# Where experts without tokens among the first 256 stand in the order of a streamed mixture of experts

## The chip, the cores and the metric

One NeuronCore of a Trainium2 chip runs the whole program. The metric is device microseconds of one execution. Beside the plain runs there is one profiled execution, whose trace gives the start and end of every instruction, what each waited for, and every DMA packet.

## The reference

One residual block over 512 tokens of width 1024, in float32. After a token mixer and a LayerNorm a hierarchical mixture of experts follows: a router picks one of 4 groups, then 2 of that group's 8 experts, so 1024 assignments fall on 32 experts.

```python
pg = softmax(xt @ w_rg + b_rg);  grp = argmax(pg)
le = (xt @ w_re + b_re).reshape(n_tok, 4, 8)[grp]
top_v, top_i = lax.top_k(le, 2)
gate = p_grp * softmax(top_v)
eid = grp * 8 + top_i
...
hb = silu(xb @ w1[e]) * (xb @ w3[e])      # w1, w3: 1024 x 512
y  = (hb @ w2[e]) * gate                  # w2: 512 x 1024, added to the token's row
out = LN2(alpha * h + sum of the two y)
```

The setup scales the router's biases up (`b_rg` by 185, `b_re` by 61), so the load is uneven. Evaluating the reference's router on its own inputs gives these tokens per expert (rows are groups, columns experts 0 to 7 of a group):

```
all 512 tokens                    first 256 tokens
 1   0   2   2   1   2   1   1     0   0   1   2   1   1   1   0
57  55  40  18  94  83  37 130    29  30  16  11  40  36  16  62
34  22  82 104  15  18 126  19    18  12  43  54   5  12  65   5
 0  11   8   5  26  15  13   2     0   7   5   4  17   8  11   0
```

Experts 1 and 24 get no token at all. Experts 0, 7 and 31 get none among the first 256, but one, one and two later.

## The kernel before, in words

Up to about 690 us the token mixer, the residual, the first LayerNorm and the router run. From there to the end the 32 experts are taken one after the other, each as one "block" b = 0 to 31; the position in the order is the block's number.

**Weights.** A block needs six chunks of 1 MB (128 partitions x 8 KB): chunks 0 to 3 hold w1 and w3, chunks 4 and 5 hold w2. `load_big` (L402) issues each chunk as one DMA from SP's queue into a ring of 17 buffers (12 named `raw`, then `rawl`, `raw`, `rawl`, `rawh`, `rawh`; in the trace a run of twelve `raw` loads is followed by these five). The queue's sequence is (b; 0 to 3), (b-1; 4, 5), (b+1; 0 to 3), (b; 4, 5) and so on. From block 3 on a load carries a condition: if the expert's final count is zero, the instruction is issued, but moves nothing.

**Lanes.** Each DMA from SP or ACT is given one of eight semaphores, in turn, by the framework (`DMAHW0` to `DMAHW7` below; I call them lanes). A DMA waits until the one before it on its lane has landed, whichever queue that one was issued from. A skipped load takes its lane and gives it back at once.

**A block.** `run` (L1393) does, in step b: `up` (L1539, h = x w1 and x w3), `gate` (L1546 on ACT, L1547 on DVE), `turn_x` of block b+1 (L1514), `down` of block b-1 (L1567), `turn` of block b (L1553 to L1557), `store_y` of block b-1 (copies L1594 and L1599, scatters L1574 on POOL). `up` and `down` are in branches on the token count: a 32-row part runs if a remainder is left (`xs`), and one or two 64-row parts (`x`) if the count is above 32 or 96. A block without tokens still goes through its transposes, gate, copies and scatters.

**The tail.** From position 25 (`RT`) on, four of the 17 buffers are taken out of the ring and used for the last LayerNorm. In step 25, behind the copies of `turn`, ACT issues four 4 KB loads of LayerNorm rows (L1622) on lanes 5, 6, 0 and 1. In step 29 ACT issues the first of four 1 MB loads of finished rows (L1689) behind all scatters so far; these take lanes 4, 6, 3 and 5.

**The order.** It is made on the chip, from the counts of the first 256 tokens (`order`, L1118), before the second half of the router has run. Every expert gets a key; its position is the number of smaller keys. The keys' parts are `seq` (group + 4 x index in the group, times 8 + 1/64, which takes the groups in turn), minus the count, and three bands: experts 0, 8 and 16 first, whatever their counts; those with tokens next; those without tokens; and last the four held for the end (`lt`, of each group the one with the fewest tokens among those that have any), whose rows go straight into the last LayerNorm.

Of the kernel before, what the change touches and what calls it, by code (L numbers as in the profile page):

```python
# [22 lines left out]
OP = mybir.AluOpType  # L23
# [5 lines left out]
T, D, NT, KD, H = 512, 1024, 4, 8, 8  # L29
E, FE = 32, 512  # L30
# [24 lines left out]
def bc(ap, n, at):  # L55

    dims = [list(d) for d in ap.ap]
    dims.insert(at, [0, n])
    return bass.AP(tensor=ap.tensor, offset=ap.offset, ap=dims)
# [201 lines left out]
class K:  # L261
# [4 lines left out]
    def consts(self, S, M, W):  # L266


        nc, a, c = self.nc, self.a, {}
        self.c = c  # L270
        v, g = nc.vector, nc.gpsimd
# [6 lines left out]
        def iota(pool, name, shape, pat, base, cm):  # L278
            t = pool.tile(shape, F32, name=name)
            g.iota(t, pattern=pat, base=base, channel_multiplier=cm, allow_small_or_imprecise_dtypes=True)  # L280
            return t
# [64 lines left out]
        q = c["seq"].rearrange("p (g j) -> p g j", g=4)  # L346
        v.tensor_scalar(c["seq"], c["seq"], 8.0 + 1.0 / 64, None, op0=OP.mult)
        v.tensor_scalar(q[:, 0:NPRE, 0:1], q[:, 0:NPRE, 0:1], -1e4, 1e3, op0=OP.add, op1=OP.mult)
        iota("jx", [128, E], [[0, 4], [1, 8]], 0, 0)
        c["onesx"] = c["ones"][:, 0:NX * E]  # L350
        c["ones_bf"] = S.tile([128, 128], BF, name="ones_bf")
        v.memset(c["ones_bf"], 1.0)
# [722 lines left out]
class Router:  # L1075
# [42 lines left out]
    def order(self):  # L1118


        nc, W, cst, v, g = self.nc, self.W, self.cst, self.nc.vector, self.nc.gpsimd
        for t in range(2):
            q = W.tile([128, 2, E], BF, name="oq")
            v.tensor_tensor(out=q, in0=bc(cst["iota"][:, 0:E], 2, 1), in1=bc(self.ek[:, :, t], E, 2), op=OP.is_equal)
            for k in range(2):
                nc.tensor.matmul(self.cps[:, NT], cst["ones_bf"], q[:, k], start=t + k == 0, stop=t + k == 2)
        gj = lambda x: x.rearrange("p (g j) -> p g j", g=4)
        f = W.tile([128, E], F32, name="of_")
        v.tensor_scalar(f, self.cps[:, NT], 0.0, None, op0=OP.is_gt)
        v.memset(gj(f)[:, 0:NPRE, 0:1], 1.0)  # L1130
        sc = W.tile([128, E], F32, name="os_")
        v.scalar_tensor_tensor(out=sc, in0=self.cps[:, NT], scalar=32.0, in1=cst["jx"], op0=OP.mult, op1=OP.add)
        ne = W.tile([128, E], F32, name="on_")
        v.tensor_scalar(ne, f, -1e6, 1e6, op0=OP.mult, op1=OP.add)
        v.tensor_tensor(out=sc, in0=sc, in1=ne, op=OP.add)
        v.memset(gj(sc)[:, 0:NPRE, 0:1], 2e6)
        mn = W.tile([128, 4], F32, name="om_")
        v.tensor_reduce(out=mn, in_=gj(sc), axis=AX.X, op=OP.min)
        lt = W.tile([128, E], F32, name="ol_")
        v.tensor_tensor(out=gj(lt), in0=gj(sc), in1=bc(mn, 8, 2), op=OP.is_equal)  # L1140
        v.scalar_tensor_tensor(out=lt, in0=sc, scalar=1e6, in1=lt, op0=OP.is_lt, op1=OP.mult)
        v.scalar_tensor_tensor(out=f, in0=f, scalar=-1024.0, in1=cst["seq"], op0=OP.mult, op1=OP.add)
        v.tensor_tensor(out=f, in0=f, in1=self.cps[:, NT], op=OP.subtract)
        v.scalar_tensor_tensor(out=f, in0=lt, scalar=4096.0, in1=f, op0=OP.mult, op1=OP.add)
        eq = W.tile([128, E, E], BF, name="oeq")
        v.tensor_tensor(out=eq, in0=bc(f, E, 1), in1=bc(f, E, 2), op=OP.is_lt)
        pos = W.tile([128, E], F32, name="op_")
        v.tensor_reduce(out=pos, in_=eq, axis=AX.X, op=OP.add)
        v.tensor_tensor(out=eq, in0=bc(pos, E, 1), in1=bc(cst["iota"][:, 0:E], E, 2), op=OP.is_equal)
        g.tensor_tensor(out=eq, in0=eq, in1=bc(cst["iota"][:, 0:E], E, 1), op=OP.mult)  # L1150
        v.tensor_reduce(out=self.ord, in_=eq, axis=AX.X, op=OP.add)
        v.tensor_copy(out=self.ordi, in_=self.ord)
# [833 lines left out]
```

## Time and profile before

| | |
|---|---|
| median of 3 runs | 1206.45 us (1206.35 to 1207.39) |
| profiled execution | 1204.72 us, of which the span from first to last instruction is 1202.9 us |
| instructions | 18,914 |
| granted TensorE clock, mean of the span | 0.938 |
| PE, DVE, ACT, POOL busy | 87%, 55%, 33%, 19% of the span |
| weight loads of the experts issued by L402 | 192 (of which 12 are skipped) |
| matmul records of `up`, 32-row parts | 1120 + 192 + 160 = 1472, that is 64 each for 23 blocks |
| matmul records of `up`, 64-row parts | 352 + 64 + 32 = 448, that is 32 each for 14 parts |

The counts of records agree with the table of tokens above: 23 experts have a remainder for the 32-row part, 8 have one 64-row part and 3 have two. Busy shares are means over stages with different limits; what the expert stage waits for is read from its own stretch of the trace. "DMA share" there is the mean busy share of the core's 16 DMA engines, and can read slightly above 1.

### The profile page before, as it was taken

The page shows a single profiled execution, that of the slowest core. Times are in us where ns is not written, and L with a number is a line of the kernel's source. Part 1 is how long each engine was busy: PE and PEld are TensorE (multiplying, and loading weights), DVE is VectorE, ACT ScalarE, POOL GpSimd, SP SyncE. Part 2 cuts the span into 40 slices and gives each one's busy share as a digit, 9 for nine tenths or more (in the row PEclk, how much of TensorE's full clock was granted, in tenths as well). Part 3 has the DMA queues.
Part 4 walks back from the last instruction along what each step waited for, and adds up shares of the span by engine and source line. Part 5 has one row for each costly group of instructions (what it writes and reads, how often), then busy time and mean ns, then how long its engine had stood idle before and what let it go on. Part 6 is the DMA issues. An engine that isn't in the chain of part 4 may idle for free. (4 is left out here: it accounts for less than half of the span.)

```text
span 1202.9 us, 18914 instructions
## 1 busy us (share of the span) xinstructions
PE 1045.7 (87%) x6866; PEld 687.0 (57%) x6866; DVE 656.7 (55%) x1392; ACT 401.1 (33%) x849; POOL 230.7 (19%) x296
## 2 busy tenths in 40 slices
PE   3999999999999999999999968888888879767853
PEld 2788688867777777767788633443443334333321
DVE  7566535367586777764485645453333323335584
ACT  6333337335545445444533121121111101122210
POOL 1000100022212322230100123232222212233301
PEclk8999999999999999999999979999989989876767
DMA  4422342621122111111647579999999999987996
GB/s 174 162 70 72 119 144 88 214 84 53 54 70 71 53 53 54 53 54 61 223 159 297 210 287 385 387 401 397 393 399 399 380 408 413 409 328 302 409 407 241
DMA packets 57930, 268.82 MB, mean 223 GB/s; under 512 B 12881, under 2 KB 17265, under 8 KB 33736
## 3 DMA queue, kind: packets, MB, share of 16 engines
q1 hardware_dynamic: 44400, 246.96, 53.8%
q0 software_dynamic: 10224, 10.88, 3.0%
q10 hardware_dynamic: 3176, 9.20, 2.1%
q8 instruction: 87, 1.43, 0.5%
q14 instruction: 43, 0.35, 0.1%
HBM read 274.23 MB, written 27.29 MB: 251 GB/s over the span
## 5 line engine op out<-in xcount | busy, mean ns | idle before, releaser
L215 PE MATMUL psi<-hTh,lo 128*128 128x512 f32 x448 | 183.7, 411 | 1.6 <-DVE lo L215 1.6
L215 PE MATMUL psi<-hTh,hi 128*128 128x512 f32 x448 | 184.2, 414 | 0.9 <-ACT hi L215 0.5
L215 PE MATMUL psi<-hTl,hi 128*128 128x512 f32 x448 | 183.9, 413 | 0.0
L1547 DVE TENSOR_TENSOR h<-h,u 128x640 f32<-128x640 f32 x32 | 26.3, 821 | 245.4 <-ACT h L1546 245.4
L215 DVE TENSOR_TENSOR lo<-raw,hi 128x1024 fp32r<-128x1024 f32 x74 | 92.4, 1249 | 79.8 <-ACT hi L215 79.6
L215 ACT CAST hi<-raw 128x1024 fp32r<-128x1024 f32 x74 | 77.4, 1046 | 108.0 <-PE psi L215 91.1
L1539 PE MATMUL u<-raw,xs 128*32 128x256 f32 x1120 | 79.9, 427 | 30.4 <-DMA raw<-in_w 28.7
L215 PEld LDWEIGHTS psi<-hTh,lo 128*128 128x128 f32 x448 | 84.9, 190 | 21.4 <-issue 3.9
L215 PEld LDWEIGHTS psi<-hTh,hi 128*128 128x128 f32 x448 | 85.1, 190 | 20.2 <-issue 2.6
L215 PEld LDWEIGHTS psi<-hTl,hi 128*128 128x128 f32 x448 | 84.7, 189 | 17.5 <-issue 2.0
L1546 ACT ACTIVATE h<-u 128x640 f32<-128x640 f32 x32 | 22.5, 704 | 200.8 <-PEq L1481 151.9
L1539 PE MATMUL u<-raw,x 128*64 128x512 f32 x352 | 80.8, 608 | 2.5 <-PEq L1479 1.4
L1539 PEld LDWEIGHTS u<-raw,xs 128*32 128x32 f32 x1120 | 37.9, 120 | 65.7 <-DMA raw<-in_w 37.6
L1574 POOL DMA_INDIRECT y_rows<-ysmall,itail x28 | 26.1, 933 | 223.1 <-DVE ysmall L1594 205.9
L1556 ACT COPY hT<-t 128x128 f32<-128x128 f32 x32 | 8.5, 266 | 176.4 <-PE t L1553 176.4
L1574 POOL DMA_INDIRECT y_rows<-ylarge,islot x56 | 57.2, 1022 | 44.4 <-ACT ylarge L1599 31.0
L215 DVE SCALAR_TENSOR_TENSOR acc<-xp,cols,acc 128x512 f32<-128x512 f32 x72 | 54.5, 758 | 5.3 <-ACT acc L215 4.1
L1567 PE MATMUL yz<-raw,hT 128*32 128x256 f32 x560 | 44.7, 459 | 14.3 <-DMA raw<-in_w 5.5
L1539 PEld LDWEIGHTS u<-raw,x 128*64 128x64 f32 x352 | 28.4, 140 | 49.3 <-issue 46.2
L1594 DVE COPY ysmall<-yz 32x256 f32<-32x256 f32 x112 | 46.7, 417 | 6.6 <-PE yz L1567 4.1
L1567 PE MATMUL y<-raw,hT 128*64 128x512 f32 x168 | 39.0, 604 | 7.2 <-PEq L1479 6.9
L1514 PE MATMUL t<-ident,mh 64*128 64x64 f32 x256 | 24.4, 243 | 23.5 <-PEq L1481 19.1
(505 smaller groups left out, 1987.6 us busy)
## 6 DMA issues: line engine op xcount, KB each, us to landing
raw<-in_w SPq DMA_DIRECT2D x144, 1024.0 KB
raw<-in_wt SPq DMA_DIRECT2D x73, 512.0 KB
rawl<-in_w SPq DMA_DIRECT2D x24, 1024.0 KB
rawh<-in_w SPq DMA_DIRECT2D x24, 1024.0 KB
raw<-in_wv SPq DMA_DIRECT2D x8, 512.0 KB
y_rows<-zero SPq DMA_DIRECT2D x8, 512.0 KB
raw<-y_rows ACTq DMA_DIRECT2D x4, 1024.0 KB
rawl<-in_wo SPq DMA_DIRECT2D x3, 1024.0 KB
```

What stands on the lines that cost most here:

```text
L215: op._ins = getattr(getattr(self.nc, op.attr), op.name)(*map(real, op.args), **{k: real(x) for k, x in op.kw.items()})
L1514: nc.tensor.transpose(self.t[0][:, k * NA:k * NA + NA], r[0][:, k * 128:k * 128 + 128], ident[0:NA, 0:NA])
L1539: self.nc.tensor.matmul(self.u[q * r:(q + 1) * r, NP if p is None else p, 0:c], x[:, k, r0:r0 + r], self.raw[b, k // 2][:, o:o + c], start ...
L1546: self.nc.scalar.activation(out=h, in_=u[:, :, 0], func=AF.Silu)
L1547: self.nc.vector.tensor_mul(out=h, in0=h, in1=u[:, :, 1])
L1556: self.nc.scalar.copy(out=x[:, n], in_=self.t[1][:, 0:128])
L1567: self.nc.tensor.matmul(y[q * r:(q + 1) * r, 0:c], t[:, i, j * r:(j + 1) * r], self.raw[b, 4 + k // 2][:, o:o + c], start=k == 0, stop=k == 3)
L1574: x = self.nc.gpsimd.indirect_dma_start(out=out, out_offset=bass.IndirectOffsetOnAxis(ap=idx, axis=0), in_=src, in_offset=None, bounds_che ...
L1594: nc.vector.tensor_copy(out=small[:, q], in_=src)
```

## The change

Experts without tokens among the first 256 lose their band behind the others. They get a key of their own, `apart` = 80.5 + 24.0625 x group + 6 x index, which lies inside the range of the keys of the experts with tokens (`seq` before, 0 to 248.5, less the count). Everything else of the order stays.

```diff
-        iota("jx", [128, E], [[0, 4], [1, 8]], 0, 0)
+        iota("apart", [128, E], [[385, 4], [96, 8]], 1288, 0)
+        v.tensor_scalar(c["apart"], c["apart"], 1.0 / 16, None, op0=OP.mult)
+        v.tensor_tensor(out=c["seq"], in0=c["seq"], in1=c["apart"], op=OP.subtract)
...
-        v.scalar_tensor_tensor(out=sc, in0=self.cps[:, NT], scalar=32.0, in1=cst["jx"], op0=OP.mult, op1=OP.add)
+        v.scalar_tensor_tensor(out=sc, in0=self.cps[:, NT], scalar=64.0, in1=cst["apart"], op0=OP.mult, op1=OP.add)
...
-        v.scalar_tensor_tensor(out=f, in0=f, scalar=-1024.0, in1=cst["seq"], op0=OP.mult, op1=OP.add)
+        v.tensor_tensor(out=f, in0=f, in1=cst["seq"], op=OP.mult)
+        v.tensor_tensor(out=f, in0=f, in1=cst["apart"], op=OP.add)
         v.tensor_tensor(out=f, in0=f, in1=self.cps[:, NT], op=OP.subtract)
```

With the counts above, the order by position is as follows, as expert(tokens of all 512). It was worked out from the formulas of `order`; positions 0 to 9 and 28 to 31 are the same in both.

```
position   before                              now
10 to 13   3(2) 12(94) 4(1) 13(83)             1(0) 3(2) 12(94) 7(1)
14 to 17   28(26) 22(126) 5(2) 21(18)          4(1) 13(83) 28(26) 22(126)
18 to 21   15(130) 29(15) 14(37) 6(1)          24(0) 5(2) 21(18) 15(130)
22 to 25   30(13) 23(19) 24(0) 1(0)            29(15) 14(37) 6(1) 31(2)
26, 27     7(1) 31(2)                          30(13) 23(19)
28 to 31   2(2) 11(18) 27(5) 20(15)            the same
```

On DVE, among the constants at the program's start (`seq` and `apart` are the tables of key parts):

```order
 L215 TENSOR_SCALAR seq<-seq 128x32
 L215 TENSOR_SCALAR seq<-seq 128x3
+L215 TENSOR_SCALAR apart<-apart 128x32
+L215 TENSOR_TENSOR seq<-seq,apart 128x32
 L215 TENSOR_TENSOR ustrict<-uincl,ident 128x128
```

Two instructions came in behind those that make `seq`; those that follow are the same, two places later.

On DVE, in `order`, before (`of_` is the key, `os_` and `om_` the choice of the four held for the end, `cps` the counts; the number behind a name is that of the buffer):

```order
L1129 TENSOR_SCALAR of__5020<-cps_4777 128x32
L1132 SCALAR_TENSOR_TENSOR os__5023<-cps_4777,jx_183 128x32
L1130 MEMSET of__5020 128x3
L1134 TENSOR_SCALAR on__5025<-of__5020 128x32
L1135 TENSOR_TENSOR os__5023<-os__5023,on__5025 128x32
L1142 SCALAR_TENSOR_TENSOR of__5020<-of__5020,seq_182 128x32
L1136 MEMSET os__5023 128x3
L1143 TENSOR_TENSOR of__5020<-of__5020,cps_4777 128x32
L1138 TENSOR_REDUCE om__5029<-os__5023 128x4
```

and now (a line of the changed file is two or three higher):

```order
L1131 TENSOR_SCALAR of__5022<-cps_4779 128x32
L1134 SCALAR_TENSOR_TENSOR os__5025<-cps_4779,apart_183 128x32
L1132 MEMSET of__5022 128x3
L1136 TENSOR_SCALAR on__5027<-of__5022 128x32
L1137 TENSOR_TENSOR os__5025<-os__5025,on__5027 128x32
L1144 TENSOR_TENSOR of__5022<-of__5022,seq_182 128x32
L1138 MEMSET os__5025 128x3
L1145 TENSOR_TENSOR of__5022<-of__5022,apart_183 128x32
L1140 TENSOR_REDUCE om__5031<-os__5025 128x4
L1146 TENSOR_TENSOR of__5022<-of__5022,cps_4779 128x32
```

One instruction more stands in the chain from the counts to the order; the rest keeps its place.

On SP, the weight loads around the four row loads of step 25, before: chunks (26; 1 to 3), (25; 4, 5), (27; 0, 1). What stands in brackets is what the DMA waits for: its lane, and PE, which must have read the buffer's last chunk.

```order
L402 DMA raw_5341<-in_w 128x2048 [waits DMAHW4_49,PE_49]
L402 DMA raw_5342<-in_w 128x2048 [waits DMAHW7_49,PE_49]
L402 DMA raw_5343<-in_w 128x2048 [waits DMAHW2_49,PE_49]
L402 DMA raw_5344<-in_w 128x2048 [waits DMAHW3_49,PE_49]
L402 DMA rawl<-in_w 128x2048 [waits DMAHW4_49,PE_49]
L402 DMA raw_4757<-in_w 128x2048 [waits DMAHW5_49,PE_49]
L402 DMA rawl<-in_w 128x2048 [waits DMAHW6_49,PE_49]
```

and now:

```order
L404 DMA raw_5344<-in_w 128x2048 [waits DMAHW4_49,PE_49]
L404 DMA raw_5345<-in_w 128x2048 [waits DMAHW7_49,PE_49]
L404 DMA raw_5346<-in_w 128x2048 [waits DMAHW2_49,PE_49]
L404 DMA raw_5347<-in_w 128x2048 [waits DMAHW3_49,PE_49]
L404 DMA rawl<-in_w 128x2048 [waits DMAHW4_49,PE_49]
L404 DMA raw_4759<-in_w 128x2048 [waits DMAHW5_49,PE_49]
L404 DMA rawl<-in_w 128x2048 [waits DMAHW6_49,PE_49]
```

Nothing moved here, nor anywhere on PE, ACT, POOL and SP: the program on these engines is the same, and so are its lanes. What moves is the expert that stands at a position, and with it which loads are skipped: chunks of positions 24 and 25 before, of positions 10 and 18 now.

## The prediction

> **What bounds the kernel now.** I read the stretch of the experts first, as a table of windows from 740 us on: busy time of each engine, granted clock, DMA share, GB/s.
>
> ```profile
> core 0: us, PE busy (x) PEld busy (x) DVE busy (x) ACT busy (x) POOL busy (x), PEclk, DMA share, GB/s
> 740.00:1050.00 310.00, 257.72 (x2271) 120.41 (x2271) 107.09 (x218) 50.13 (x99) 83.77 (x86) 0.96 1.02 399
> 1050.00:1055.00 5.00, 2.96 (x34) 1.69 (x35) 2.95 (x6) 0.00 (x0) 0.06 (x1) 0.80 0.97 393
> 1055.00:1060.00 5.00, 4.12 (x53) 1.95 (x51) 1.26 (x3) 1.83 (x4) 2.81 (x3) 0.86 0.85 323
> 1060.00:1065.00 5.00, 2.96 (x36) 1.68 (x40) 1.60 (x4) 0.70 (x1) 1.06 (x2) 0.82 0.94 360
> 1065.00:1070.00 5.00, 3.96 (x29) 1.53 (x21) 2.93 (x6) 0.43 (x2) 0.00 (x0) 0.50 0.56 224
> 1070.00:1075.00 5.00, 1.54 (x16) 1.11 (x20) 1.46 (x4) 2.10 (x4) 3.70 (x4) 0.84 0.84 296
> 1075.00:1080.00 5.00, 3.19 (x33) 1.58 (x25) 3.27 (x7) 0.85 (x2) 0.66 (x2) 0.82 1.01 411
> 1080.00:1085.00 5.00, 1.41 (x9) 1.11 (x9) 1.76 (x4) 1.78 (x3) 3.37 (x4) 0.53 0.46 178
> 1085.00:1090.00 5.00, 4.58 (x37) 2.29 (x40) 3.70 (x7) 1.83 (x4) 1.56 (x2) 0.50 0.09 16
> 1090.00:1140.00 50.00, 40.97 (x350) 18.06 (x343) 25.59 (x37) 12.63 (x24) 18.13 (x17) 0.76 1.01 402
> ...
> 1145.00:1150.00 5.00, 1.88 (x27) 0.84 (x29) 2.38 (x2) 2.11 (x6) 0.00 (x0) 0.85 0.90 339
> 1150.00:1180.00 30.00, 17.85 (x169) 7.36 (x165) 24.10 (x35) 3.72 (x8) 2.74 (x4) 0.61 1.01 421
> ```
>
> The DMA engines are full (1.02 at 399 GB/s) for 310 us, and again from 1090 us on. PE is not: 258 of 310 us. So a weight chunk of 1 MB (1.049 million bytes) takes 1.049/0.399 = 2.63 us, and six of them, 15.8 us, are the price of a block. The one hole of size is 1050 to 1090 us. Next the waits of SP's queue, us in total, times, longest, and its issues of weight loads:
>
> ```profile
> SPq L402 <- DMA raw<-in_w: 194.6, 96, 4.4
> ...
> SPq L402 <- DMA raw<-y_rows: 26.1, 4, 17.5
> SPq L1652 <- DMA raw<-in_w: 19.1, 1, 19.1
> ...
> SPq L402 <- DMA raw<-in_rows: 9.0, 1, 9.0
> ...
> 1015.75 30.09 SPq L402 DMA_DIRECT2D raw<-in_w  x12
> 1048.01 0.09 SPq L402 DMA_DIRECT2D rawl<-in_w  x1
> 1050.48 0.08 SPq L402 DMA_DIRECT2D raw<-in_w  x1
> 1053.56 0.07 SPq L402 DMA_DIRECT2D rawl<-in_w  x1
> 1056.30 2.61 SPq L402 DMA_DIRECT2D rawh<-in_w  x2
> 1061.06 14.09 SPq L402 DMA_DIRECT2D raw<-in_w  x12
> 1078.49 0.08 SPq L402 DMA_DIRECT2D rawl<-in_w  x1
> 1088.62 0.34 SPq L402 DMA_DIRECT2D raw<-in_w  x1
> ...
> 1186.41 2.89 SPq L1652 DMA_DIRECT2D out<-h1s  x4
> ```
>
> SP mostly waits for an earlier weight load to land: its lane. Loads of 0.07 to 0.09 us are skipped ones; 1048.01 is chunk (24, 0). They still wait for their lanes, about 2.6 us each, and put nothing in flight: the reserve of loads under way melts. In the middle of that, SP stands still from 1078.49 to 1088.62, 9.0 us of it for the row loads of step 25, whose lane chunk (27, 0) comes next on. ACT's rows (gates, copies of `turn`, the row load):
>
> ```profile
> 1029.40 0.59 ACT L1557 COPY hT<-t 128x512 f32<-128x512 f32 x1
> ...
> 1056.04 0.59 ACT L1557 COPY hT<-t 128x512 f32<-128x512 f32 x1 [0.53 <-PE t L1555]
> 1062.21 0.70 ACT L1546 ACTIVATE h<-u 128x640 f32<-128x640 f32 x1 [4.62 <-PEq L1481]
> ...
> 1072.86 0.70 ACT L1546 ACTIVATE h<-u 128x640 f32<-128x640 f32 x1 [1.47 <-PEq L1481]
> ...
> 1082.08 0.70 ACT L1546 ACTIVATE h<-u 128x640 f32<-128x640 f32 x1 [0.88 <-PEq L1481]
> ...
> 1086.72 0.59 ACT L1557 COPY hT<-t 128x512 f32<-128x512 f32 x1 [1.21 <-PE t L1555]
> 1086.90 0.49 ACTq L1622 DMA_DIRECT2D raw<-in_rows  x1
> ```
>
> ACT gives out the rows only behind block 25's `turn`. The last weights are seen by SP just before its output store at 1186.41, 16.5 us ahead of the span's end. The load stream sets the end; no load can be saved by an order, but a hole in it can.
>
> **The sum.** It is made against the profiled execution, 1204.72 us (span 1202.9 and 1.8 outside), and carried over to the median of 1206.45, 1.73 above it.
>
> *The hole goes.* Shares missing from 1.02 in the eight windows of 1050 to 1090: 0.05 + 0.17 + 0.08 + 0.46 + 0.18 + 0.01 + 0.56 + 0.93 = 2.44, times 5 us = 12.2 us. (By bytes: 991 GB/s times 5 us missing from 399, over 399: 12.4.) Of these 4.75 lie ahead of 1080, where blocks 24 and 25 are skipped back to back, and 7.45 behind it, where SP stands. Positions 24 and 25 now hold six real loads each, so both parts go: -12.2.
>
> *Two holes come in,* at positions 10 and 18, each alone. Each again lets six lanes go empty, but seven loaded blocks lie between them. No row shows a lone skip. The first skipped block's four chunks alone, 1050 to 1065, cost 0.30 x 5 = 1.5 us; half of the pair's cost is 2.4. I take the middle, 1.9 each: +3.8. The pair's second block ran into a reserve already melted, so 2.4 is more likely too high than too low. A lone skip could cost nothing, if three loads in flight were enough; a gain from it is excluded, since it moves no bytes.
>
> [...]
>
> *The row loads' stop stays, its cover comes back.* Lanes 5, 6, 0 and 1 belong to the rows, so when SP comes to (27, 0) the lanes 2, 3, 4 and 7 carry (26, 2), (26, 3), (25, 4) and (25, 5): four real loads, 4 x 2.63 = 10.5 us of cover. Before, the last two were skipped and DMA ran dry at about 1082 (178/399 x 5 = 2.2 us behind 1080). How long SP will stand is read from blocks before: the six blocks ahead of position 25 are now experts 5, 21, 15, 29, 14 and 6, which stood ahead of position 22 before. Rows issue 0.18 us after the copy's start and SP goes on at 1088.62 - 1086.72 = 1.90 after it. At block 22 that moment is 1056.04 + 1.90 = 1057.94; SP was at (24, 0) at 1048.01, and three loads later, where the lanes would now hold it, at 1055.9: a stop of 2.0 us. At block 20, two behind the expert with 130 tokens, 1031.30 against 1015.75 + 7.9: 7.7 us. Both are under 10.5, so nothing runs dry. Since four loads are under way and not seven, I take 0.5 us (the window at 0.94 lost 0.4). Upper end: 7.7, with 2 us for a `down` of block 24 and 4 us of lateness, and 1 us to start again, less 10.5, is 4.2. Lower end 0.
>
> *The instructions.* Their nearest row is one of the chain itself:
>
> ```profile
> L1142 DVE SCALAR_TENSOR_TENSOR of__5020<-of__5020,seq x1: 183/183/183, 663.8 to 663.8; 128x32 f32<-128x32 f32 x1
> ```
>
> One of about 0.19 us is added in `order`, and two at the start, beside vector work that PE doesn't wait for there; if that cover were gone, 0.4 us. The one in the chain: +0.2, between 0 (the first load by the order issues only some 40 us later) and 0.2.
>
> *PE's work* is the same: an empty block's step costs PE the same at each place. By the gates above the two steps took 10.65 and 9.22 us, against 15.8 us of loads that fall away: after each empty position PE is some 10 us further behind the loads. What takes that up is time in which PE waits for loads, here between 833 and 1050 us:
>
> ```profile
> PE u L1539 <- DMA raw<-in_w: 15.5, 11, 2.3
> ...
> PE yz L1567 <- DMA raw<-in_w: 1.8, 2, 1.4
> PE u L1539 <- DMA rawl<-in_w: 1.7, 1, 1.7
> ```
>
> 19.0 us against 19.9: nearly all is swallowed, and expert 7's small block, now at 13, leaves some 5 us more (15.8 against a step of about 10). So 0, with an upper end in the rivals. The row loads of step 29 held SP for 17.5 us and cost one window at 0.90 (0.6 us); positions 28 to 31 are unchanged, and I leave that.
>
> Sum: -12.2 + 3.8 + 0.5 + 0.2 = -7.7. The profiled execution would be 1197.0, the median **1198.7 us**. Own range: from 1194.2 (all 12.2 gained) to 1206.45 - 12.2 + 4.8 + 4.2 + 0.6 = 1203.9.
>
> **Rivals.**
>
> *The stop isn't covered* (0.13). SP comes to (27, 0) and DMA runs dry for as long as before. For it: four lanes, not eight, feed the engines at that place in any order. Against: the cover of 10.5 us. Then the 7.45 stay, with 3.8 for 4.75 and 0.2: 1205.7, inside 0.2% of before.
>
> *PE comes late, slower than before* (0.07). If none of the two steps' 20 us is taken up, the stop is 2.0 + 20 = 22, and 22 + 1 - 10.5 = 12.5 us run dry where I take 0.5: 1210.7. It gets slower than before once 7.7 + 0.5 us run dry, that is, from a stop of 17.7 us, 16 of the 20 left over. Against it stand the 19.0 us of waits; for it, that many of these lie in the blocks right after the heavy ones, and:
>
> ```profile
> L1539 PE MATMUL u<-raw,xs x1120: 376/379/637, 701.2 to 1174.6; 128*32 128x256 f32 x187
> ...
> 1086.61 5.56 PE L1539 MATMUL u<-raw,xs 128*32 128x256 f32 x64
> ```
>
> Behind the empty steps the granted clock was 0.53 and 0.50, and these 64 matmuls took 5.56 us, which at 376 instead of 637 ns each would be 3.3: up to 2.3 us more per empty position. That is 4.6 us of lateness in all, under the 16 needed. [...]
>
> *The order isn't what I worked out* (0.06). If the counts of the first 256 tokens differ on the chip, the empty positions fall elsewhere; if they stay at the end, nothing is gained: 1206.5. For the counts speak the numbers of matmul records, which come from the same router.
>
> *Lone skips and the stop cost nothing* (0.08): 1194.2 to 1196.
>
> **How the numbers follow.** 0.66 for my forecast, and the rivals as given. About 0.2%, 2.4 us, is what a measurement of this kernel can tell from no change: 1204.0 and 1208.9. My case and the last rival are faster: 0.74. The uncovered stop and the other order are within: 0.19. PE late is slower: 0.07. The range runs from 1194.2 to 1205.7, from the whole hole gained to the uncovered stop.
>
> **What would show it.** In the changed profile SP's loads of under 0.1 us stand near 812 and 934 us and not at 1048 to 1078; the windows there dip for some 15 us by 0.1 to 0.2 and no window after 1050 falls under 0.8 until the last load; the wait for the row loads is still there, up to 8 us, with the share near 1; the output store comes near 1178.7 and the span ends 16.5 us later. I am wrong if SP waits for PE at L402 in 850 to 1050, if a window near 1060 to 1080 falls to 0.5, or if the dips at the two skips cost more than 2.4 us each.

## The result, and the profile after

The changed kernel takes **1197.93 us** (median of 4 runs, 1195.99 to 1199.78) against 1206.4 for the kernel before on the same chip: a ratio of 0.9925, 95% interval 0.9910 to 0.9941. That is 8.5 us less; 7.7 were forecast. The profiled execution took 1195.99 us (span 1194.1, granted clock 0.945). A second chip, on which the kernel before takes 1218.8 us, shows no gain that can be measured; that is the subject of half the experiments.

The windows of the changed kernel in the form of those of before (busy time per engine, granted clock, DMA share, GB/s):

```profile
740.00:1050.00 310.00, 255.57 (x2198) 121.39 (x2195) 111.12 (x226) 51.55 (x101) 86.78 (x89) 0.93 1.02 397
810.00:815.00 5.00, 4.57 (x22) 1.96 (x24) 1.39 (x4) 1.40 (x3) 2.68 (x3) 1.00 1.02 418
...
820.00:825.00 5.00, 5.00 (x30) 2.03 (x26) 0.00 (x0) 0.57 (x1) 0.00 (x0) 1.00 1.02 418
...
1060.00:1065.00 5.00, 4.04 (x25) 1.69 (x25) 3.14 (x7) 0.33 (x2) 0.95 (x2) 1.00 1.01 383
1065.00:1070.00 5.00, 3.49 (x64) 1.82 (x56) 0.00 (x0) 1.64 (x4) 2.79 (x3) 1.00 0.88 318
1070.00:1075.00 5.00, 4.27 (x60) 3.01 (x64) 3.81 (x8) 1.53 (x4) 0.18 (x1) 1.00 1.02 389
1075.00:1080.00 5.00, 3.22 (x54) 1.87 (x46) 1.65 (x3) 1.06 (x2) 3.06 (x4) 1.00 0.77 307
1080.00:1085.00 5.00, 3.69 (x40) 1.67 (x40) 3.00 (x6) 0.70 (x1) 2.86 (x3) 0.78 0.89 331
```

The hole of 12.2 us is gone. What is left of it is 0.14 + 0.25 + 0.13 shares of 5 us, 2.6 us, around the row loads. At and behind the skipped loads the share is 1.02 (first skip); no window of 5 us at the second falls under 0.99.

SP's issues (start, time, engine and line, tensor), from two stretches, and the start of its output store:

```profile
810.18 0.09 SPq L404 DMA_DIRECT2D raw<-in_w  x1
812.66 0.08 SPq L404 DMA_DIRECT2D rawl<-in_w  x1
...
937.59 0.07 SPq L404 DMA_DIRECT2D raw<-in_w  x1
...
1178.78 3.24 SPq L1655 DMA_DIRECT2D out<-h1s  x4
```

The skipped loads (0.07 to 0.09 us) now stand near 812 and 934, and the store at 1178.78, where 1178.7 was forecast. The waits of SP's queue from 740 us on (total, times, longest), and then what PE's own queue waits for between 833 and 1050 us in weight loads, which is all that is left of 19.0 us before:

```profile
SPq L404 <- DMA raw<-in_w: 134.8, 61, 7.8
SPq L404 <- PEq L1484: 53.0, 14, 9.6
...
SPq L404 <- PE y L1570: 15.1, 3, 8.1
...
SPq L404 <- DMA raw<-in_rows: 5.6, 1, 5.6
```

```profile
PE yz L1570 <- DMA raw<-in_w: 0.4, 1, 0.4
```

The same wait of SP for PE's queue before, over the same stretch:

```profile
SPq L402 <- PEq L1481: 18.3, 7, 7.4
```

So PE has changed sides: it no longer waits for weights, and SP now waits for PE to free buffers, 53.0 us at L1484 (18.3 before) and 15.1 at L1570 (0.2 before). The DMA share stays at 0.99 or more up to 1065 us all the same: between 800 and 1050 us a `raw` load took 17.8 us from issue to landing at the median, nearly seven times the 2.64 us that a chunk takes at 397 GB/s, so an estimated six or seven loads were under way.

### The profile page after: what moved, and what is told of

Same layout as the page of the kernel before. It is cut to its first block, busy times and chain, and to the rows that moved or that the text cites. A ratio compares the mean times of both kernels' runs of the same rounds, so it can differ in the third digit from the quotient of the medians.

```text
span 1194.1 us, 18917 instructions
## 1 busy us (share of the span) xinstructions
PE 1043.8 (87%) x6866; PEld 690.0 (58%) x6866; DVE 657.4 (55%) x1395; ACT 401.0 (34%) x849; POOL 230.8 (19%) x296
## 5 line engine op out<-in xcount | busy, mean ns | idle before, releaser
L215 ACT CAST hi<-raw 128x1024 fp32r<-128x1024 f32 x74 | 77.4, 1047 | 108.0 <-PE psi L215 91.3
L1542 PE MATMUL u<-raw,xs 128*32 128x256 f32 x1120 | 78.5, 426 | 16.5 <-DMA raw<-in_w 15.0
L1542 PE MATMUL u<-raw,x 128*64 128x512 f32 x368 | 83.8, 604 | 2.6 <-PEq L1482 1.5
L1549 ACT ACTIVATE h<-u 128x640 f32<-128x640 f32 x32 | 22.6, 705 | 181.4 <-PEq L1484 139.4
L1542 PEld LDWEIGHTS u<-raw,xs 128*32 128x32 f32 x1120 | 41.2, 121 | 47.9 <-DMA raw<-in_w 19.1
L1570 PE MATMUL yz<-raw,hT 128*32 128x256 f32 x560 | 42.2, 439 | 12.9 <-PEq L1522 6.8
L215 POOL TENSOR_TENSOR rk<-ssk,mhalf 128x4 f32<-128x4 f32 x8 | 9.6, 1194 | 183.1 <-DVE ssk L215 168.6
L1570 PE MATMUL y<-raw,hT 128*64 128x512 f32 x152 | 39.7, 666 | 5.8 <-PEq L1482 5.8
```

The costliest lines, as they stand in the source:

```text
L215: op._ins = getattr(getattr(self.nc, op.attr), op.name)(*map(real, op.args), **{k: real(x) for k, x in op.kw.items()})
L1542: self.nc.tensor.matmul(self.u[q * r:(q + 1) * r, NP if p is None else p, 0:c], x[:, k, r0:r0 + r], self.raw[b, k // 2][:, o:o + c], start ...
L1549: self.nc.scalar.activation(out=h, in_=u[:, :, 0], func=AF.Silu)
L1570: self.nc.tensor.matmul(y[q * r:(q + 1) * r, 0:c], t[:, i, j * r:(j + 1) * r], self.raw[b, 4 + k // 2][:, o:o + c], start=k == 0, stop=k == 3)
```

## The experiments

The runs went to chips of two kinds. "The first chip" below stands for those on which the kernel before takes 1206.4 to 1206.7 us, as in the result; on "the second chip" it takes 1218.7 to 1218.8 us. Ratios are always to the kernel before on the same chip.

### The code with the old order; second chip

```diff
-        iota("apart", [128, E], [[385, 4], [96, 8]], 1288, 0)
+        iota("apart", [128, E], [[385, 4], [96, 8]], 40000, 0)
...
+        v.memset(c["apart"][:, 24:25], 2503.0)
```

> The changed code with other key constants: the keys of experts without tokens lie above all others (base 2500, expert 24 first), so that the order is that of before: 24, 1, 7 and 31 at positions 24 to 27. It keeps the added vector instructions, plus one more at the start. If the order alone makes the gain (my theory), this is before again: 1206.4 within 0.3%, with the hole at 1050 to 1090 us back and a stop of about 9 us for the row loads. If anything in the changed code itself matters, the time lies between 1198 and 1206.

1219.31 us, ratio 1.0008 (0.9988 to 1.0027): the added instructions cost nothing that can be measured, which here means less than some 3 us. The hole and SP's stop for the row loads are back, the stop at 13.7 us and not at about 9. Since the changed kernel turned out to gain nothing on this chip either, this run alone doesn't show that the order makes the gain; the two moves of expert 24 below do.

### The changed kernel again; first chip, then second

```diff
(no edit)
```

> The changed kernel, unchanged, to have its own time beside the runs below on the same chip. On the chip of the first four runs the kernel before took 1218.7 us, with a row stop of 13.7 us instead of 9.0, and PE's small steps 1 to 2 us longer. Theory 1 (the change's gain is the hole of the pair, and PE's lateness is free as long as three or more loads are in flight): ratio to before 0.991 to 0.995, about as on the first chip (0.9925), with the row stop at 8 to 10 us and 3 to 6 us lost there. Theory 2 (a slower PE makes the order's gain vanish, because the loads wait for PE): 0.997 to 1.001.

1197.66 us, ratio 0.993 (0.9912 to 0.9948). The gain is repeated.

> The changed kernel, unchanged, as the measure for the three runs beside it: ratio to before 0.991 to 0.995 as in its two measurements so far (0.9925, 0.993), if the chip's TensorE steps are those of these two; 0.993 to 0.998 by either theory on a chip like that of the first four runs, where small steps take 1 to 2 us more.

On the second chip: 1220.29 us, ratio 1.0008 (0.9990 to 1.0026). No gain. I had given 0.993 to 0.998 for this chip, and that was wrong. The windows tell where it went, first with the old order (the run above), then with the new one:

```profile
1050.00:1060.00 10.00, 7.88 (x81) 3.40 (x77) 1.37 (x4) 1.83 (x4) 3.86 (x4) 0.89 0.89 357
1060.00:1070.00 10.00, 8.41 (x109) 5.21 (x109) 4.64 (x9) 2.53 (x5) 1.90 (x2) 0.83 0.72 275
1070.00:1080.00 10.00, 5.76 (x49) 3.24 (x45) 4.09 (x8) 1.02 (x3) 1.96 (x2) 0.66 0.43 161
1080.00:1090.00 10.00, 5.95 (x45) 3.44 (x45) 5.12 (x11) 2.58 (x6) 3.86 (x4) 0.66 0.67 271
1090.00:1100.00 10.00, 5.90 (x49) 3.25 (x53) 5.52 (x11) 3.99 (x8) 5.72 (x6) 0.66 0.15 28
```

```profile
800.00:850.00 50.00, 40.98 (x273) 18.02 (x271) 14.97 (x30) 7.60 (x15) 11.62 (x12) 0.96 0.94 362
...
950.00:1000.00 50.00, 40.79 (x287) 17.92 (x287) 16.00 (x31) 7.50 (x15) 11.93 (x13) 0.90 0.91 352
...
1090.00:1100.00 10.00, 7.02 (x111) 4.24 (x109) 2.80 (x5) 2.61 (x6) 2.98 (x3) 1.00 0.12 43
1100.00:1110.00 10.00, 4.00 (x66) 2.34 (x64) 2.66 (x6) 1.61 (x4) 5.93 (x6) 0.94 0.70 256
```

Old order: 0.13 + 0.30 + 0.59 + 0.35 + 0.87 shares of 10 us, 22.4 us, all at the pair and the row loads. New order: 0.08 x 50 = 4.0 us at the first skip, 0.11 x 50 = 5.5 at the second, and 0.90 x 10 + 0.32 x 10 = 12.2 at the row loads: 21.7 us. The hole has been cut in three, but is as large as before, by one profiled execution of each. The one at the row loads is what the rival "PE comes late" had priced at 12.5 us, with a stop of 22. SP's wait there is 18.8 us in this run, for which that rival's own formula gives 9.3:

```profile
SPq L404 <- PEq L1484: 128.3, 28, 12.2
...
SPq L404 <- DMA raw<-in_rows: 18.8, 1, 18.8
```

Why PE is later on this chip is seen where both chips do the same: the same order, block 9, on the first chip (kernel before) and on the second (the old order with the new code). The 64 matmuls of `up` and the transposes that follow:

```profile
828.81 3.66 PE L1539 MATMUL u<-raw,xs 128*32 128x256 f32 x64
832.79 0.68 PE L1514 MATMUL t<-ident,mh 64*128 64x64 f32 x8 [0.32 <-PEq L1481]
```

```profile
835.52 3.66 PE L1543 MATMUL u<-raw,xs 128*32 128x256 f32 x64
841.58 0.68 PE L1518 MATMUL t<-ident,mh 64*128 64x64 f32 x8 [2.40 <-PEq L1485]
```

The matmuls take the same 3.66 us, but PE's sequencer comes out of the branches behind them 2.40 us later instead of 0.32. Summed over 833 to 1050 us for this place in the code, and beside it what PE still waits for weights on the second chip (on the first it was 19.0 us):

```profile
PE t L1514 <- PEq L1481: 6.3, 11, 2.7
```

```profile
PE t L1518 <- PEq L1485: 28.3, 10, 4.3
PE y L1571 <- DMA raw<-in_w: 2.0, 2, 1.2
...
PE yz L1571 <- DMA raw<-in_w: 0.5, 1, 0.5
```

That is 22.0 us more at this place. PE waits for its sequencer at other places too: 5.0, 3.7, 2.6 and 0.8 us on the first chip, 2.5, 0.8, 0.8 and 0.8 on the second. Over all of them it is 33.2 against 18.4, 14.8 us more, and 16.5 us less waiting for weights: the slack that was to swallow PE's lateness is nearly used up on this chip before anything is moved. What the pause consists of, and why it is longer on one chip, no run here shows.

### Both empty experts next to each other in the middle; second chip

```diff
+        v.memset(c["apart"][:, 24:25], 88.0)
```

Positions 10 and 11 are empty now.

> As the changed kernel, but expert 24 gets the key 88, so that both empty experts stand back to back at positions 10 and 11. Theory 1, the pair's cost lies in standing back to back, wherever that is (12 of 14 chunks in a row put nothing in flight): the windows around 820 to 850 lose 3 to 5 us of DMA share, and the time is 1201 to 1203. Theory 2, a pair costs only where PE has caught up with the loads: no dip, 1198 within 1.5. In both the stop for the row loads stays covered, since positions 24 and 25 hold loads.

1221.88 us, ratio 1.0020 (0.9999 to 1.0042), which can't be told from the changed kernel's 1.0008 on this chip.

```profile
830.00:840.00 10.00, 8.61 (x49) 3.60 (x49) 4.55 (x9) 1.09 (x3) 0.50 (x1) 1.00 0.26 104
840.00:850.00 10.00, 6.60 (x82) 3.71 (x76) 3.10 (x6) 2.14 (x4) 3.36 (x4) 0.93 0.28 82
...
870.00:1050.00 180.00, 144.73 (x1319) 70.87 (x1319) 59.48 (x115) 28.49 (x57) 48.91 (x50) 0.88 1.02 396
```

The pair alone makes a hole of 0.76 + 0.74 shares of 10 us, 15.0 us, far from any row load, three times the most that was expected. Between 810 and 860 us SP waits 14.7, 6.4 and 5.3 us for PE at three lines, 26.4 us in all. That fits the program: a skipped load moves nothing, but like any other it waits until PE has read what its buffer held before, and its buffer counts as taken until PE has passed its block. Two empty blocks make 12 skipped loads, and the ring has 17 buffers, which leaves few for real loads. That the ring, and not the lateness of PE alone, makes the hole so long was not tested by itself. Both theories had the row loads' stop covered, and it was not: SP stands for 12.0 us there, and 0.27 + 0.49 shares of 10 us are missing from 1090 to 1110, 7.6 us. Together the two holes, 22.6 us, come to about what the changed kernel loses, 21.7.

### Three or five places apart; second chip

```diff
+        v.memset(c["apart"][:, 24:25], 108.0)
```

With 108.0 expert 24 stands at position 13; the second run has 130.0, which puts it at 15.

> Expert 24 moves from position 18 to 13, three places behind the other empty one, with 3(2) and 12(94) between. Theory 1 (an empty position makes TensorE 10 to 16 us late, a small block brings back some 5 us and one of 94 tokens nothing; the ring of 17 buffers hides one empty position and no more): the second one comes before the first is worked off, so 10 or more us of lateness stand above what the ring hides: 5 to 12 us slower than the changed kernel, as a hole in the DMA share within 30 us of the second skip, with waits of SP for PE above 80 us. Theory 2 (the pair's hole comes only from the lack of any real load between the two, which six or more real loads between them mend): within 1.5 us of the changed kernel.

1221.79 us, 1.5 us above the changed kernel beside it; ratio 1.0007 (0.9988 to 1.0026), against 1.0008 there. (The ratios on record are not the quotients of the medians, which would be 1.0024 here; both say no more than that the difference is below some 3 us.)

> Expert 24 at 15, five places behind the other, with 3(2), 12(94), 7(1) and 4(1) between. Theory 1: the three small blocks bring back some 15 us, so little or nothing is left: 0 to 4 us slower than the changed kernel, less than with 13, and no window under 0.7 ahead of 1050. Theory 2: within 1.5 us of the changed kernel and the same as 13.

1219.74 us, ratio 1.0007 (0.9988 to 1.0026), 0.6 us below the changed kernel. In time both came out as theory 2 had it, and in the trace 13 came out as theory 1 had it:

```profile
850.00:900.00 50.00, 34.53 (x317) 17.17 (x313) 18.98 (x36) 10.03 (x20) 14.89 (x17) 0.88 0.76 293
...
1090.00:1100.00 10.00, 6.98 (x89) 4.05 (x85) 4.83 (x10) 1.62 (x4) 2.25 (x4) 0.83 0.39 154
1100.00:1110.00 10.00, 5.72 (x64) 2.81 (x56) 1.15 (x2) 1.61 (x3) 5.83 (x6) 0.80 0.78 302
```

A hole of 0.26 x 50 = 13.0 us stands behind the second skip, as expected, but the one at the row loads shrinks from 12.2 to 0.63 x 10 + 0.24 x 10 = 8.7 us. My estimate, which no run shows by itself, is that PE catches up while DMA stands early on, and is less late at the row loads. Neither theory had that: as far as these runs show, on this chip the order only chooses where the loads wait for PE. (With 15 the share fell to 0.68 from 890 to 900 us, where theory 1 had said none under 0.7.)

### Expert 24 at position 25, then at 24; first chip

```diff
+        v.memset(c["apart"][:, 24:25], 200.0)
```

200.0 puts expert 24 at position 25, 193.0 in the second run at 24. With 25 the loads (25; 4, 5), which stand ahead of the stopped (27, 0), are skipped; with 24 they are real.

> Only expert 24 moves, from position 18 to position 25 (expert 31 goes to 24): its loads (25; 4, 5), the two issued right ahead of the one that the rows stop, are now skipped, so the stop is covered by two real loads, 5.3 us, not four. Theory 1 (what covers the stop is the real loads under way): against the changed kernel the cover is 5.3 us less, and the stop some 5 us longer, since the stream has gone ahead by six skipped loads (15.8 us) while PE saves less: 6 to 11 us slower than the changed kernel, which is the time of before or above it (ratio to before 0.998 to 1.004), and most of it as one hole in the 15 us behind the stop. Theory 2 (the reserve doesn't matter, the stop is paid for in part however many loads are under way): 3 to 6 us slower, the same as the run with expert 24 at 24.

1206.68 us, ratio 1.0005 (0.9989 to 1.0020): 9.0 us above the changed kernel.

> As the run with expert 24 at 25, but at 24: the skipped loads are (24; 0 to 3) and (24; 4, 5), and (25; 4, 5) are real again, so four real loads stand ahead of the stopped one. Theory 1: the stop gets longer by some 5 us as the stream is 15.8 us ahead and PE's empty step takes 10 to 12, but the cover is 10.5 us: 2 to 6 us slower than the changed kernel and 4 to 6 us faster than with expert 24 at 25. Theory 2: the same as with expert 24 at 25, within 2 us.

1201.34 us, ratio 0.9968 (0.9955 to 0.9981): 3.7 us above it, 5.3 below the other. First with 25, then with 24:

```profile
SPq L405 <- DMA raw<-in_rows: 8.8, 1, 8.8
...
1075.00:1080.00 5.00, 0.00 (x0) 0.00 (x0) 0.00 (x0) 1.16 (x3) 3.34 (x4) 0.59 0.78 299
1080.00:1085.00 5.00, 4.49 (x40) 2.50 (x40) 2.96 (x5) 0.61 (x1) 0.09 (x1) 0.50 0.12 43
1085.00:1090.00 5.00, 4.83 (x73) 2.86 (x69) 2.58 (x5) 1.83 (x4) 2.10 (x3) 0.88 0.23 33
```

```profile
SPq L405 <- DMA raw<-in_rows: 12.0, 1, 12.0
...
1075.00:1080.00 5.00, 3.71 (x52) 2.35 (x44) 1.08 (x2) 1.78 (x3) 2.84 (x3) 0.86 0.73 271
1080.00:1085.00 5.00, 3.65 (x55) 2.42 (x59) 4.33 (x9) 1.91 (x4) 0.89 (x2) 1.00 0.12 40
1085.00:1090.00 5.00, 4.06 (x65) 2.46 (x58) 2.50 (x6) 0.70 (x1) 3.78 (x5) 1.00 0.84 312
```

With 25 the wait is the shorter one, 8.8 against 12.0 us, and yet costs more: (0.24 + 0.90 + 0.79) x 5 = 9.7 us against (0.29 + 0.90 + 0.18) x 5 = 6.9. What covers a stop is the real loads under way, two or four. Theory 1 held in both times and in their difference; the stop itself, 5.9 us in the changed kernel beside them, grew by 2.9 and 6.1 us, where some 5 had been expected in both. And as the empty position alone moves, the position is shown to be what the gain on this chip hangs on. One empty position at 25 is enough to lose all of it, though the other still stands at 10; what the pair's standing back to back costs by itself on this chip was not run.

### The row loads from another queue

```diff
-                act.dma_start(out=x, in_=kk.a["rows"][row:row + 1, :])
+                g.dma_start(out=x, in_=kk.a["rows"][row:row + 1, :])
```

The four 4 KB loads then take none of the eight lanes. In the kernel before, second chip:

> The kernel before, with one edit: the four 4 KB row loads of step 25 go through POOL's queue and no longer take lanes of SP's loads; the order stays that of before. My theory (SP's stop for the row loads, with its cover skipped, is 7.45 us of the 12.2): the windows of 1080 to 1090 fill up, the pair's 4.75 us stay, 1199 to 1200. Rival, SP would next wait for PE to free the buffer or for the ring cut to 13: the hole stays, 1204 to 1207.

1213.63 us, ratio 0.9955 (0.9934 to 0.9975): in the ratio this is the theory's 1199 to 1200 of 1206.4, and the rival's 1204 and more is excluded. The share from 1080 to 1100 is full, as expected, and the hole of the two empty blocks stays: 0.09 + 0.24 + 0.91 shares of 10 us, 12.4 us, are missing from 1050 to 1080. The trace is that of the run's slowest execution, 1218.16 us, in which another 10.3 us are missing from 1100 to 1160 (3.0 in the run with the old order above), so it doesn't account for the whole gain in time. In the changed kernel, second chip, twice:

> The changed kernel with the same edit on the row loads. In the changed profile the windows from 1065 to 1085 lose 0.14, 0.25 and 0.13 of share, 2.6 us. Theory, these come from the lanes taken by the row loads: they fill up, 1195 to 1196. Rival, they come from PE being late (SP waits for PE some 59 us between 833 and 1050): nothing changes, 1197 to 1199.

1211.25 us, ratio 0.9942 (0.9917 to 0.9967), against 1.0008 for the changed kernel.

> The changed kernel with the four 4 KB row loads alone issued from POOL's queue; the 1 MB loads of finished rows stay on ACT's. Theory 1 (the row stop's 2.6 us of missing share are on the path): 2 to 3 us below the changed kernel. Theory 2 (what the stream gains before 1140 is given back at its end, as when both kinds of loads were moved: there the output store stayed at 1178.3 although no share was missing ahead of 1165): within 1 us of it, with the share falling earlier than 1175 and the store still near 1178.

1213.98 us, ratio 0.9961 (0.9940 to 0.9983), some 6 us below the changed kernel beside it, so theory 1's direction came true with more than its 2 to 3 us, which had been taken from the first chip's stop. SP's wait for the row loads, 13.7 us with the old order and 18.8 with the new one on this chip, is gone in all three. In the changed kernel it had a hole of 12.2 us on this chip, so half of that is given back. The second skip costs 0.14 x 50 = 7.0 us instead of 5.5, and in the last run the stop at the loads of finished rows now loses 0.42 x 10 + 0.17 x 10 = 5.9 us, 3.8 more than the 0.17 + 0.04 shares of 10 us in the changed kernel beside it.

```profile
1140.00:1150.00 10.00, 8.62 (x13) 3.31 (x13) 3.00 (x7) 3.62 (x7) 3.58 (x4) 0.50 0.60 220
1150.00:1160.00 10.00, 8.25 (x106) 4.33 (x106) 3.10 (x6) 1.30 (x2) 0.35 (x1) 0.81 0.85 328
```

So I moved both kinds of loads, on the first chip:

```diff
-        return self.nc.scalar.dma_start(out=self.y[t % 2], in_=self.y_dram[...
+        return self.nc.gpsimd.dma_start(out=self.y[t % 2], in_=self.y_dram[...
```

> The changed kernel, with the four 4 KB row loads and the four 1 MB loads of finished rows issued from POOL's queue, so that they take none of the lanes and no weight load waits for them. In the run with the row loads alone moved the stop at the row loads was gone, and the stop at the finished rows still stood (21.2 us, with a DMA share of 0.71 over 20 us, so 6 us lost). Theory 1 (both stops are paid because tiny or late loads hold lanes): ratio to before 0.985 to 0.990, 3 to 7 us below the changed kernel, with the wait of SP for either load gone. Theory 2 (with the lanes free, the last weights wait for PE instead, which is late by then): no more than 1 us below the run with the row loads alone moved (0.9942).

1197.36 us, ratio 0.9925 (0.9903 to 0.9947): the same as the changed kernel, and theory 1's 3 to 7 us did not come. Both stops are gone, and no share is missing up to 1165. Then, in this run and in the changed kernel beside it:

```profile
1165.00:1170.00 5.00, 2.82 (x32) 1.01 (x32) 4.04 (x10) 0.00 (x0) 0.95 (x2) 0.80 0.83 342
1170.00:1175.00 5.00, 3.91 (x36) 1.27 (x32) 3.81 (x4) 0.70 (x1) 0.11 (x1) 0.52 0.45 185
1175.00:1180.00 5.00, 2.62 (x29) 1.51 (x29) 3.25 (x3) 2.30 (x6) 0.00 (x0) 0.82 0.24 95
```

```profile
1170.00:1175.00 5.00, 4.13 (x34) 1.58 (x35) 4.50 (x4) 0.28 (x1) 0.00 (x0) 0.50 0.99 406
1175.00:1180.00 5.00, 2.81 (x25) 1.50 (x27) 2.56 (x2) 2.30 (x6) 0.00 (x0) 0.50 0.44 179
```

The stream runs out earlier, but step by step over 15 us, and PE still starts block 30's `down` when its weights come, at 1170.81 us here and at 1170.76 in the first profile of the changed kernel; the output store starts at 1178.30 and 1177.66. The gain is lost in a ragged end. What makes it ragged (some of the 16 engines having more left to do than others, or the order in which the queues are served) is open. So is the row loads' move alone on the first chip, which wasn't run: by the windows it would be worth at most the 2.6 us of its stop, less what comes back behind it.

## Why the prediction was right, and where it wasn't

The time, 1198.7 against 1197.93, lay well inside the range on the chip of the result. By its steps:

- **The hole goes, -12.2.** Right on the first chip: the windows of 1050 to 1090 are full but for the row loads' share. Moving one of the two empty experts back to 25 brings the time of before back.
- **Two lone skips, +3.8.** Mis-sized: no share is missing there, so 0. Between 740 and 1050 us DMA moved 397 GB/s instead of 399 at the same share, which is 1.6 us at most. The lower bound of the step, that few loads in flight are enough, was the truth on this chip; on the second, where PE has no slack, the two cost 4.0 and 5.5 us. My value came from a pair's first block, which had a reserve that was already shrinking.
- **The row loads' stop, +0.5.** The stop lay in the forecast 2.0 to 7.7 us, at 5.6, but cost 2.6. The cover was reckoned as four whole loads. The last of them run at a share of 0.77 to 0.89, and the oldest, issued at 1058.81 us, landed 16.2 us later, when SP had stood for 1 of its 5.6 us (it goes on at 1079.60). The 1 us to start again is what the kernel before shows: SP goes on at 1088.62 us, and the share is 0.00 from 1089.0 to 1089.5 and 0.46 in the half microsecond behind. By "stop plus 1 us less cover" the costs would be 0, 2.5 and 4.5 us for the changed kernel, 24 and 25; measured were 2.6, 6.9 and 9.7. On the second chip it is 9.3 against 12.2. The formula is short by 3 to 5 us where it gives more than nothing.
- **PE's lateness, 0.** Right in time, and right in what takes it up: PE's waits for weights fell from 19.0 to 0.4 us. The sign that I had named for its failure, SP waiting for PE, came true without a loss. It should have been a share under 1 while SP waits. The margin was nearly nothing, and on the second chip it was not there.
- **Instructions, +0.2.** Too small to be seen (ratio 1.0008, 0.9988 to 1.0027, on the second chip).
- **What I had left out:** in the profiled executions the first gate came 0.97 us earlier (705.86 against 706.83), and the end behind the output store was 15.3 us and not 16.5. These 2.2 us lie outside the change, and within what profiled executions of one kernel differ by (the second profile of the changed kernel has 17.4 us behind the store).
- **What doesn't add up.** From the first gate to the output store the profiled executions differ by 6.7 us (479.58 and 472.92), but -12.2 and +2.6 make -9.6. So some 3 us are lost elsewhere, where no term of the sum stood. The 1.6 us at most between 740 and 1050 are part of it; from 1130 to 1160, and in the last 4 to 6 us ahead of the store, where the share is 0.40 instead of 0.73, some 0.5 us each are missing more than before. The rest is open; it is about what a share given to two places can tell over so long a stretch.

So the mechanism of the gain was right, and that the sum came out so near was partly luck: two terms erred against each other, the lone skips by +3.8 too much and the stop by +2.1 too little, and some 3 us of loss that had no term stand against 2.2 us that the two profiles happened to differ by. The rival that ends slower, "PE comes late", was dismissed on the strength of 19.0 us of waits in one trace. On the second chip its mechanism ran as described. That its hole came out as priced (12.2 against 12.5 us) is luck, though: the stop was 18.8 us and not 22, and the formula short by 3. The whole came out at no change and not slower, because the old order loses as much there.

## What to carry to other kernels

Here work that was skipped under a condition still passed through ring, lanes and the consumer's step, and the stream got ahead by the bytes saved only as far as the consumer's own slack reached: 8.5 us were gained where PE waited 19.0 us for weights, and nothing that could be measured where it waited 2.5. So set that slack beside the lateness that each skipped block makes (an estimated 10 us here), and see what other chips leave of it. Place skipped blocks several blocks ahead of any wait that stops the issuing queue: on the first chip expert 24 at 25 or 24 cost 9.0 or 3.7 us more than at 18. Two back to back made a hole of 15.0 us where two apart made 4.0 and 5.5, but that gained no time that could be measured on the second chip, and wasn't tried on the first. Count as cover for such a wait only the loads that really move, less one or two (with whole loads the formula was short by 3 to 5 us, at some 2.6 us a load). When a queue begins to wait for another engine, look at the share of the transfers before calling it a loss: SP's waits for PE of 28.9 us at L1484 and 15.1 at L1570 between 833 and 1050 us went with a share of 0.99 or more.

## What the runs showed of the hardware

- With four skipped loads in a row, and so at most four real ones in the eight lanes, DMA stays full on the first chip: 1.02 and 418 GB/s from 820 to 825 us, right behind four skipped chunks.
- Two chips differ by 1% in time with one program (1206.7 and 1218.8 us). The same 64 matmuls take 3.66 us on both; what differs in the traces is the pause of PE's sequencer at branches, 0.32 and 2.40 us at the same place, 18.4 and 33.2 us over 833 to 1050 us. That this pause makes the whole 1% wasn't tested.
- The granted clock fell in the first empty step of the changed kernel, to 0.70 and 0.62 from 835 to 845 us, and not in the run with expert 24 at 25, where it is 1.00 over the same stretch. A pause of PE of 2.94 us came ahead in the one, of 2.66 us in the other (first the changed kernel):

```profile
838.39 3.68 PE L1570 MATMUL y<-raw,hT 128*64 128x512 f32 x8 [2.94 <-PEq L1482]
```

```profile
835.18 1.94 PE L1571 MATMUL y<-raw,hT 128*64 128x512 f32 x8 [2.66 <-DMA raw<-in_w]
```

  The same eight matmuls took 3.68 and 1.94 us. In the first case PE's last matmuls end at 835.45 us, and the granted clock reads 1.00 until 837.0 and 0.5 from there to about 843.7: it fell 1.5 us into the pause, so the pause's whole length can't be what decided. A single pause of 2.94 us went with the halving here, beside a smaller one of 0.32 us just ahead of it, which the other run has too.
